# Multi-query attention on one core: TensorE's rounds of scores and value products follow the five-step period of the vector steps

## The chip, the cores and the metric

The kernel runs on one core of a Trainium2 chip. The metric is the device time in microseconds of one execution. Engine names in the profile: PE is TensorE (PEld its weight loads), ACT is ScalarE, DVE is VectorE, POOL is GpSimd, SP is SyncE.

## The reference

Attention with 16 query heads and one shared key and value head, for 8 batches of 1,024 tokens with head size 64:

```python
q = q.transpose(0, 2, 1, 3)                       # 8 x 16 x 1024 x 64
scores = np.matmul(q, k.transpose(0, 1, 3, 2)) / np.sqrt(head_dim)
weights = np.exp(scores - np.max(scores, axis=-1, keepdims=True))
weights = weights / np.sum(weights, axis=-1, keepdims=True)
attn_out = np.matmul(weights, v)                  # back to 8 x 1024 x 16 x 64
```

## The kernel before

The work is cut into 1,024 **steps** (`STEPS`). A step is one pair of heads, one chunk of 512 queries and one tile of 128 keys. Eight steps over the eight key tiles make a **chunk**; two chunks make a pair of heads, eight pairs a batch.

In a step, `scores` (L241) runs two matmuls on TensorE (L247), one for each head, which use the two halves of the array's rows side by side. They fill a PSUM tile `sc` of 128 keys by 1,024. The pool `scp` has three such tiles, so the scores of step u wait until the exponentials of step u-3 have been read out of theirs. No maximum is subtracted: a check at the end of each batch tests that the row sums stay in bounds.

The exponentials of a step are made by one of two units. In most steps ScalarE makes them in one instruction (L260). Every fifth step (`VE_EVERY = 5`, steps 10, 15, 20 and so on to 1005) is a **vector step**: VectorE makes them in five instructions (`vector_exp`, L206). The first (L211) reads the scores; the others (L217, L227, L235, L237) follow from the list `pend`, from which each step takes up to two entries. The fifth (L237) is put off until the next vector step. A vector step leaves its weights as three terms, each with its own scaled copy of the values.

The **value products** (`values`, L307, matmul L318) then multiply the weights, as the stationary operand, with the values (65 columns; the last one sums the weights). One **group** is one head's block of 128 queries; a chunk has eight groups. A group's sum runs over the eight key tiles, one product for a step by ScalarE and three for a vector step. A chunk with one vector step has 10 products a group, with two it has 12; three chunks in five have two. Seven groups share a PSUM bank (`ot`), of which there are two. When a bank is full, `late` notes it; VectorE then inverts the sums (`inverse`, L263) and scales the outputs (`finish`, L272), and SyncE's queue stores them. Some of the finishes end a batch and run the check too (L360, L366, L370).

The order on each engine is the order in which the program is written (`tc.manual_schedule`). The main loop (L448) goes by rounds of two steps: two steps' scores on TensorE, then two groups of value products, `LAG` = 18 steps behind. So a vector step is now the first, now the second step of a round, with a pattern that repeats every ten steps. From step 1012 (`HURRY`) on a round takes up to four groups. At the head of a round's value part, banks noted in the round before are put into `pend`. The last eight groups are done key tile by key tile at the end (`last_values`, L331, matmul L344), in two banks from the same pool. `after` (L392) issues the next batch's loads and transposes on POOL's and SP's queues.

Of the kernel before, what the change touches and what calls it, by code (L numbers as in the profile page):

```python
# [21 lines left out]
C0 = 0.9833984375  # L22
C3 = 0.163818359375
CS = 2.1471603163479376
VE_EVERY = 5


@with_exitstack
def attention_main(ctx, tc, q, k, v, out, flag):
# [14 lines left out]
    NKT = S // P  # L44
    QCH = 512
    NCH = S // QCH
    HP = H // 2
    NP = B * HP
    NQB = QCH // P
    GRP = 2 * NQB  # L50
    NG = NP * NCH * GRP
    GB = 7
# [25 lines left out]
    kv = {}  # L78
    q16 = {}
    qt = {}  # L80
    wt = {}
    osb = {}
    ot = {}
    pend = []
    product = []
    late = []
# [48 lines left out]
    def bank(name):  # L135
        return op.tile([P, 512], FP32, tag="ot", name=name)
# [32 lines left out]
    def first_q(ps, p, cs):  # L169
        for c in cs:  # L170
            nc.tensor.matmul(  # L171
                ps[:, c * P : (c + 1) * P],
                q16[("first", p)][:, c, :],
                ident16,
                is_transpose=True,
                start=True,
                stop=True,
            )
# [62 lines left out]
    def scores(p, c, j, by_vector):  # L241
# [17 lines left out]
        wt[(p, c, j)] = [(w, 0)]  # L259
        nc.scalar.activation(out=w, in_=sc, func=EXP, scale=escale, bias=math.log(CS))  # L260

    def inverse(o, g0, n):
        nc.vector.reciprocal(out=rec_all[:, g0 : g0 + n], in_=o[:, 0:n, D])  # L263

    def finish(o, g0, n):

        rec = rec_all[:, g0 : g0 + n]
        i0 = g0 % (OCH * GRP)
        if i0 == 0:
            osb[0] = osbp.tile([P, OCH * GRP, D], FP32, tag="osb", name=f"osb{g0}")  # L270
        ob = osb[0]
        nc.vector.tensor_tensor(  # L272
            out=ob[:, i0 : i0 + n, :],
            in0=o[:, 0:n, 0:D],
            in1=rec.unsqueeze(2).broadcast_to([P, n, D]),
            op=ALU.mult,
        )
        while stored[0] < g0 + n:
            e = stored[0]
            e += GRP // 2 if e >= NG - GRP else GRP  # L280
            if e > g0 + n:
                break
            store(ob, stored[0], e)
            stored[0] = e
        per = HP * NCH * GRP
        if g0 + n == NG:
            check(g0 - GRP // 2, NG, ok_all[:, B:])
        elif checked[0] < B and g0 + n >= min((checked[0] + 1) * per, NG - GRP):
            e = min((checked[0] + 1) * per, NG - GRP)
            b = checked[0]  # L290
            check(b * per, e, None, ok_all[:, b : b + 1])
            checked[0] += 1

    def store(ob, g0, g1):
        p, c = divmod(g0 // GRP, NCH)
        b, hp = divmod(p, HP)
        q0 = c * QCH + g0 % GRP // 2 * P
        j0 = g0 % (OCH * GRP)
        n = g1 - g0
        nc.sync.dma_start(  # L300
            out=out[b, q0 : q0 + n // 2 * P, 2 * hp : 2 * hp + 2, :].rearrange(
                "(qb p) h d -> p qb (h d)", p=P
            ),
            in_=ob[:, j0 : j0 + n, :].rearrange("p (qb h) d -> p qb (h d)", h=2),
        )

    def values(p, c, g):  # L307

        b = p // HP
        qb, hh = divmod(g, 2)  # L310
        gg = (p * NCH + c) * GRP + g
        if gg % GB == 0:
            ot[0] = bank(f"ot{gg}")[:, 0 : GB * 72].rearrange("p (g f) -> p g f", f=72)
        o = ot[0]
        vp = kv[b]["vp"]
        terms = [(j, w, i) for j in range(NKT) for w, i in wt[(p, c, j)]]
        for n, (j, w, i) in enumerate(terms):
            nc.tensor.matmul(  # L318
                o[:, gg % GB, 0 : D + 1],
                w[:, hh, qb * P : (qb + 1) * P],  # L320
                vp[:, i, j, 0 : D + 1],
                start=(n == 0),
                stop=(n == len(terms) - 1),
            )
        if gg % GB == GB - 1 or gg == NG - GRP - 1:
            late.append((o, gg - gg % GB, gg % GB + 1))
        if g == GRP - 1:
            for j in range(NKT):
                del wt[(p, c, j)]

    def last_values():  # L331

# [39 lines left out]
    LAG = 2 * NKT + 2  # L372
    STEPS = NP * NCH * NKT
    PSTEPS = NCH * NKT
    BATCH = 2
    LAST_VE = (STEPS - 2 * NKT) // VE_EVERY * VE_EVERY
    HURRY = STEPS - NKT - 4

    def to_vector(u):
        return u % VE_EVERY == 0 and NKT <= u <= LAST_VE  # L380

    def step(u):
        p, r = divmod(u, PSTEPS)
        c, j = divmod(r, NKT)
        scores(p, c, j, to_vector(u))
        for _ in range(2):
            if pend:
                pend.pop(0)()
        if product and u >= LAST_VE + 2 and not pend:
            product.pop()()  # L390

    def after(u):  # L392
        p, r = divmod(u, PSTEPS)
        b, hp = divmod(p, HP)
        if u == 1:
            first_q(turned[0], 0, range(NKT // 2, NKT))
            first_q_out(turned[0], 0, range(NKT // 2, NKT), nc.vector.tensor_copy)
        if r == 7 and p + 1 < NFIRST:
            turned[p + 1] = bank(f"qps{p + 1}").bitcast(FP16)
            first_q(turned[p + 1], p + 1, range(NKT))  # L400
            first_q_out(turned[p + 1], p + 1, range(NKT), nc.vector.tensor_copy)
        if b + 1 < B:
            at = hp * PSTEPS + r - 3 * PSTEPS
            if at == 0:
                load_kv(b + 1)
                load_v(b + 1)
            if 0 <= at < 2 * NKT and at % 2 == 0:
                load_q(b + 1, at // 2)
            at -= PSTEPS
            if 0 <= at < 2 * NKT and at % 2 == 0:  # L410
                turn_q(b + 1, at // 2)
            at -= PSTEPS
            if at == 4:
                prep_k(b + 1)
            if at == 8:
                prep_v(b + 1)

    with tc.manual_schedule():
        load_kv(0)
        load_q_first(0)  # L420
        make_identity(nc, ident)
        for p in range(1, NFIRST):
            load_q_first(p)
        load_v(0)
        for c in range(NKT):
            load_q(0, c)
        for t in vps:
            for i, ci in enumerate((1.0, C0, C3)):
                nc.gpsimd.memset(t[:, i, :, D : D + 1], ci)
        nc.vector.tensor_copy(out=ident16, in_=ident)  # L430
        nc.vector.memset(ones, 1.0)
        kps = bank("kps0").bitcast(FP16)
        turned[0] = bank("qps0").bitcast(FP16)
        lo, hi = range(NKT // 2), range(NKT // 2, NKT)
        q0 = q16[("first", 0)]
        nc.scalar.copy(out=q0[:, 0 : NKT // 2, :], in_=qf[:, 0 : NKT // 2, :])  # L436
        first_k(kps, 0)
        first_q(turned[0], 0, lo)
        first_q_out(turned[0], 0, lo, nc.scalar.copy)
        first_k_out(kps, 0)  # L440
        first_k(kps, 1)
        first_k_out(kps, 1)
        nc.vector.tensor_copy(out=q0[:, NKT // 2 :, :], in_=qf[:, NKT // 2 :, :])
        prep_v(0)
        for c in range(NKT):
            turn_q(0, c)
        nxt = 0
        for u0 in range(0, STEPS, BATCH):  # L448
            us = range(u0, u0 + BATCH)
            for u in us:  # L450
                step(u)
            for f in late:
                pend.insert(0, lambda f=f: inverse(*f))
                pend.insert(min(2, len(pend)), lambda f=f: finish(*f))
            del late[:]
            for _ in range(2 * BATCH):
                if u0 < HURRY:
                    ready = nxt < u0 + BATCH - LAG
                else:
                    ready = nxt < STEPS - GRP and nxt // GRP * NKT + NKT + 4 <= u0  # L460
                if ready:
                    pa, ra = divmod(nxt, PSTEPS)
                    values(pa, *divmod(ra, NKT))
                    nxt += 1
            for u in us:
                after(u)
        assert nxt == STEPS - GRP
        assert not product
        for f in pend:
            f()  # L470
        for f in late:
            inverse(*f)
            finish(*f)
        last_values()
        okm = chkp.tile([P, 1], FP32, tag="okm", name="okm")
        nc.vector.tensor_reduce(out=okm, in_=ok_all, axis=AX.X, op=ALU.min)
        cnt = bank("cnt")[0:1, 0:1]
        nc.tensor.matmul(cnt, okm, ones, start=True, stop=True)
        nc.vector.tensor_scalar(
            out=flag, in0=cnt, scalar1=P - 0.5, scalar2=None, op0=ALU.is_lt  # L480
        )
# [120 lines left out]
```

## Time and profile before

| | |
|---|---|
| Median of 3 runs | 782.43 us (781.96 to 783.74) |
| The profiled execution's own time | 783.46 us |
| Its span, first to last instruction | 781.5 us |
| ScalarE (ACT) busy | 762.5 us, 98% |
| VectorE (DVE) busy | 728.9 us, 93% |
| TensorE (PE) busy | 728.7 us, 93% |
| Granted TensorE clock, mean | 0.990 |
| Exponentials on ScalarE | 824, mean 1,062 ns |
| Vector steps | 200 |

The page is of one profiled execution. A row of a group of instructions gives its line, engine and operation, output and input, then the count, and behind the bar the busy time in us, the mean time of one in ns, and the idle time of the engine just before such instructions with what ended most of it. Exponentials follow each other so closely that one starts before the profile's end of the one before, so busy time over count is less than the mean. A timeline row gives start and length in us and merges instructions of a kind that follow without a gap.

### The profile page before, as it was taken

To read this page: it belongs to the slowest core of one execution; us is meant where nothing else is said; L and a number is where in the kernel's file an instruction comes from. 1 tells how busy PE (TensorE), PEld (TensorE's weight loads), DVE (VectorE), ACT (ScalarE), POOL (GpSimd) and SP (SyncE) were. 2 spreads that over 40 slices of the span, in tenths; PEclk is the share of its full clock that TensorE was granted. 3 is DMA by queue.
4 is the path that set the end of the run, shared out by engine and by line. 5 is a ranking of instruction groups with operands and counts; after the bars stand their busy time and mean duration, and the time that the engine had idled before them with its cause. 6 is when DMAs were issued, how large, how long until landed. Compare 5 with 4: busy or idle time off the path is not lost.

```text
span 781.5 us, 30669 instructions
## 1 busy us (share of the span) xinstructions
PE 728.7 (93%) x13474; PEld 474.1 (61%) x13474; DVE 728.9 (93%) x1349; ACT 762.5 (98%) x827; POOL 65.9 (8%) x99
## 2 busy tenths in 40 slices
PE   5999999999999999999999999999999999999996
PEld 2566666656666666666656666666666666666665
DVE  3899999999999999999999999999999999999992
ACT  7999999999999999999999999999999999999996
POOL 4210002100011002010020100201002100000000
PEclk8899999999999999999999999999999999999999
DMA  9949118582193813756155552556417373111113
GB/s 169 146 93 164 55 44 157 97 136 57 29 170 76 154 33 76 150 103 115 45 91 123 124 95 56 90 128 115 101 42 125 89 149 71 51 35 55 43 43 84
DMA packets 168633, 73.84 MB, mean 94 GB/s; under 512 B 93744, under 2 KB 161328, under 8 KB 168496
## 3 DMA queue, kind: packets, MB, share of 16 engines
q1 hardware_dynamic: 148864, 53.76, 32.5%
q0 software_dynamic: 18576, 17.57, 14.8%
q8 instruction: 106, 1.74, 1.0%
q10 hardware_dynamic: 1056, 0.52, 0.3%
q14 instruction: 31, 0.25, 0.1%
HBM read 37.75 MB, written 33.55 MB: 91 GB/s over the span
## 4 chain that ended last, share of the span: by engine, by line
ACT 38%; DVE 21%; PE 21%; issue 19%; DMA 1%; DVEq 0%; ACTq 0%
ACT wt L260 38%; PE ot L318 11%; PE sc L247 9%; DVE we L211 8%; DVE osb L272 3%; DVE we L237 3%; DVE mm L235 3%; DVE m L217 2%; DVE we L227 2%; DVE rec_all L263 1%; DMA qf<-in_q_dram 1%; PE otl L344 0%; DVE both L366 0%; DVE ok_all L370 0%; DVE ge L360 0%
## 5 line engine op out<-in xcount | busy, mean ns | idle before, releaser
L260 ACT ACTIVATE wt<-sc 128x1024 f16<-128x1024 f32 x824 | 760.0, 1062 | 7.4 <-PE sc L247 6.1
L318 PE MATMUL ot<-vp,wt 128*128 128x65 f16 x6528 | 418.4, 194 | 0.6 <-issue 0.6
L318 PEld LDWEIGHTS <-wt 128*128 128x128 f16 x6528 | 325.8, 98 | 114.8 <-issue 114.8
L247 PE MATMUL sc<-qt,k2t 64*128 64x512 f16 x2048 | 352.8, 386 | 41.2 <-ACT wt L260 29.1
L318 PE MATMUL ot<-vp,we 128*128 128x65 f16 x4800 | 352.2, 193 | 0.0
L318 PEld LDWEIGHTS <-we 128*128 128x128 f16 x4800 | 250.0, 97 | 30.6 <-issue 30.6
L211 DVE TENSOR_SCALAR we<-sc 128x1024 int16<-128x1024 f32 x200 | 243.6, 1218 | 23.2 <-PE sc L247 22.1
L247 PEld LDWEIGHTS <-k2t 64*128 64x128 f16 x2048 | 93.2, 94 | 149.0 <-issue 111.0
L237 DVE TENSOR_TENSOR we<-we,mm 128x1024 f16<-128x1024 f16 x200 | 136.9, 685 | 0.0
L235 DVE TENSOR_TENSOR mm<-m 128x1024 f16<-128x1024 f16 x200 | 136.5, 683 | 0.0
L272 DVE TENSOR_TENSOR osb<-ot,rec_all 128x448 f32<-128x448 f32 x146 | 90.5, 620 | 4.2 <-DVE rec_all L263 0.2
L217 DVE TENSOR_SCALAR m<-we 128x1024 int16<-128x1024 int16 x200 | 85.8, 429 | 0.0
L227 DVE TENSOR_SCALAR we<-we 128x1024 int16<-128x1024 int16 x200 | 83.5, 418 | 0.0
L104 POOL DMA_DIRECT2D vp<-in_v_dram x8 | 7.5, 936 | 388.5 <-PE ot L318 388.4
L121 POOL DMA_DIRECT2D q<-in_q_dram x64 | 35.0, 571 | 26.7 <-DMA qt<-q 22.9
L263 DVE RECIPROCAL rec_all<-ot 128x7 f32<-128x7 f32 x146 | 28.6, 196 | 8.7 <-PE ot L318 8.6
L190 POOL TENSOR_SCALAR k16d<-knat 128x512 f16<-128x512 f32 x14 | 21.4, 1537 | 134.7 <-DMA knat<-in_k_dram 134.7
L202 DVE TENSOR_SCALAR vp<-vp 128x512 f16<-128x512 f16 x16 | 3.9, 286 | 2.0 <-DMA vp<-in_v_dram 2.0
L155 PE MATMUL kps<-ident,k 128*64 128x128 f16 x16 | 1.3, 314 | 4.5 <-DVE k L146 4.5
L184 DVE COPY qt<-qps 128x512 f16<-128x512 f16 (+1 forms) x2 | 1.1, 554 | 3.3 <-PE qps L171 3.3
L155 PEld LDWEIGHTS <-k 128*64 128x64 f16 x16 | 0.8, 159 | 4.7 <-DVE k L146 4.7
L436 ACT ACT_TABLE_LOAD x1 | 1.3, 1283 | 1.9 <-issue 1.9
(29 smaller groups left out, 22.2 us busy)
## 6 DMA issues: line engine op xcount, KB each, us to landing
out_dram<-osb SPq DMA_DIRECT2D x127, 256.0 KB, 2.4
q<-in_q_dram POOLq DMA_DIRECT2D x56, 256.0 KB, 8.8
knat<-in_k_dram SPq DMA_DIRECT2D x7, 256.0 KB, 4.1
q<-in_q_dram POOLq DMA_DIRECT2D x8, 192.0 KB, 8.0
vp<-in_v_dram POOLq DMA_DIRECT2D x8, 128.0 KB, 4.4
qt<-q SPq DMA_TRANSPOSE x64, 3.9
qf<-in_q_dram ACTq DMA_DIRECT2D x2, 256.0 KB, 4.4
knat<-in_k_dram SPq DMA_DIRECT2D x2, 128.0 KB, 3.8
```

Of the source, the lines that this page charges most:

```text
L121: nc.gpsimd.dma_start(out=q16[(b, c)], in_=q[b, c * P : (c + 1) * P, h0:, :].rearrange("p h d -> p (h d)"),)
L190: nc.gpsimd.tensor_scalar(out=k16d[:, :, i, :], in0=st["knat"], scalar1=kscale, scalar2=None, op0=ALU.mult)
L211: nc.vector.tensor_scalar(out=t, in0=sc, scalar1=15.0 * 1024, scalar2=0.0, op0=ALU.add, op1=ALU.max)
L217: lambda: nc.vector.tensor_scalar(out=m.bitcast(I16), in0=t, scalar1=0x3FF, scalar2=0x3C00, op0=ALU.bitwise_and, op1=ALU.bitwise_or,)
L227: lambda: nc.vector.tensor_scalar(out=w3[:, 0].bitcast(I16), in0=t, scalar1=0x7C00, scalar2=None, op0=ALU.bitwise_and,)
L235: pend.append(lambda: nc.vector.tensor_tensor(out=m2, in0=m, in1=m, op=ALU.mult))
L237: lambda: nc.vector.tensor_tensor(out=w3[:, 2], in0=w3[:, 1], in1=m2, op=ALU.mult)
L247: nc.tensor.matmul(sc[:, hh, :], k2t[r : r + 64, j * P : (j + 1) * P], qt[b][r : r + 64, p % HP, c * QCH : (c + 1) * QCH], start=True, sto ...
L260: nc.scalar.activation(out=w, in_=sc, func=EXP, scale=escale, bias=math.log(CS))
L263: nc.vector.reciprocal(out=rec_all[:, g0 : g0 + n], in_=o[:, 0:n, D])
L272: nc.vector.tensor_tensor(out=ob[:, i0 : i0 + n, :], in0=o[:, 0:n, 0:D], in1=rec.unsqueeze(2).broadcast_to([P, n, D]), op=ALU.mult,)
L318: nc.tensor.matmul(o[:, gg % GB, 0 : D + 1], w[:, hh, qb * P : (qb + 1) * P], vp[:, i, j, 0 : D + 1], start=(n == 0), stop=(n == len(terms ...
```

## The change

Three things change. First, the rounds no longer have two steps each. `DEAL` and `DEAL_AT` place the end of a round behind steps 1, 2 and 4 of each five, counted from a vector step: the vector step and the next one make a round, one step alone the second, the last two the third. Second, the rounds' value work is no longer counted in groups. `values` returns a list of single products, and `plan` works out how many products shall have been made by each round's end, so that the three rounds of a period have the same share of five groups; a group can be cut by the next round's scores. At the end of a period one group more is made than before at the same step. Third, `HURRY` is 1010 instead of 1012, and from there on rounds of two steps with up to four whole groups take a chunk's groups up two steps earlier than before.

```diff
+DEAL = (1, 1, 0, 1, 0)
+DEAL_AT = 1
 VE_EVERY = 5
...
-    def values(p, c, g):
+    def values(gg):
...
-        for n, (j, w, i) in enumerate(terms):
+        def one(n, j, w, i):
+            last = n == len(terms) - 1
             nc.tensor.matmul(
...
+        return [lambda n=n, t=t: one(n, *t) for n, t in enumerate(terms)]
...
-    BATCH = 2
-    HURRY = STEPS - NKT - 4
+    HURRY = STEPS - NKT - 6
...
+    def plan():
+        upto = [0]
+        for g in range(STEPS):
+            many = sum(to_vector(g // GRP * NKT + j) for j in range(NKT))
+            upto.append(upto[-1] + NKT + 2 * many)
+        due = {}
+        for u in range(STEPS):
+            if u >= HURRY:
+                if u % 2:
+                    due[u] = None
+                continue
+            n, i = divmod(u - DEAL_AT, len(DEAL))
+            if DEAL[i]:
+                at = DEAL_AT + len(DEAL) * (n + sum(DEAL[: i + 1]) / sum(DEAL)) - LAG
+                at = max(at, 0.0)
+                g = int(at)
+                due[u] = round(upto[g] + (at - g) * (upto[g + 1] - upto[g]))
+        return due
...
-        for u0 in range(0, STEPS, BATCH):
-            us = range(u0, u0 + BATCH)
-            for u in us:
-                step(u)
+        for u in range(STEPS):
+            step(u)
+            us.append(u)
+            if u not in due:
+                continue
+            new = []
             for f in late:
-                pend.insert(0, lambda f=f: inverse(*f))
-                pend.insert(min(2, len(pend)), lambda f=f: finish(*f))
+                new += [lambda f=f: inverse(*f), lambda f=f: finish(*f)]
+            if len(new) == 2:
+                new[1:1] = pend[:1]
+                del pend[:1]
+            pend[:0] = new
             del late[:]
-            for _ in range(2 * BATCH):
-                if u0 < HURRY:
-                    ready = nxt < u0 + BATCH - LAG
-                else:
-                    ready = nxt < STEPS - GRP and nxt // GRP * NKT + NKT + 4 <= u0
-                if ready:
-                    pa, ra = divmod(nxt, PSTEPS)
-                    values(pa, *divmod(ra, NKT))
-                    nxt += 1
+            if due[u] is not None:
+                while made < due[u]:
+                    if not todo:
+                        todo = values(nxt)
+                        nxt += 1
+                    todo.pop(0)()
+                    made += 1
+            else:
+                for _ in range(4):
+                    if not todo and nxt < STEPS - GRP and nxt // GRP * NKT + NKT + 3 <= u:
+                        todo = values(nxt)
+                        nxt += 1
...
```

More of the change, by code (lines that the diff above doesn't have):

```diff
@@ L305, in store @@
         )
-    def values(p, c, g):
-        b = p // HP
+    def values(gg):
+        p, c = divmod(gg // GRP, NCH)
+        g = gg % GRP
         qb, hh = divmod(g, 2)
-        gg = (p * NCH + c) * GRP + g
         if gg % GB == 0:
@@ L314, in values @@
         o = ot[0]
-        vp = kv[b]["vp"]
+        vp = kv[p // HP]["vp"]
         terms = [(j, w, i) for j in range(NKT) for w, i in wt[(p, c, j)]]
-        for n, (j, w, i) in enumerate(terms):
+        def one(n, j, w, i):
+            last = n == len(terms) - 1
             nc.tensor.matmul(
@@ L322, in values @@
                 start=(n == 0),
-                stop=(n == len(terms) - 1),
+                stop=last,
             )
[L325 to L329, printed above, removed]
+            if not last:
+                return
+            if gg % GB == GB - 1 or gg == NG - GRP - 1:
+                late.append((o, gg - gg % GB, gg % GB + 1))
+            if g == GRP - 1:
+                for x in range(NKT):
+                    del wt[(p, c, x)]
+        return [lambda n=n, t=t: one(n, *t) for n, t in enumerate(terms)]
     def last_values():
@@ L446, in attention_main @@
             turn_q(0, c)
-        nxt = 0
-        for u0 in range(0, STEPS, BATCH):
-            us = range(u0, u0 + BATCH)
-            for u in us:
-                step(u)
-            for f in late:
-                pend.insert(0, lambda f=f: inverse(*f))
-                pend.insert(min(2, len(pend)), lambda f=f: finish(*f))
-            del late[:]
-            for _ in range(2 * BATCH):
-                if u0 < HURRY:
-                    ready = nxt < u0 + BATCH - LAG
-                else:
-                    ready = nxt < STEPS - GRP and nxt // GRP * NKT + NKT + 4 <= u0
-                if ready:
-                    pa, ra = divmod(nxt, PSTEPS)
-                    values(pa, *divmod(ra, NKT))
-                    nxt += 1
-            for u in us:
-                after(u)
+        nxt = made = 0
+        todo = []
+        due = plan()
+        us = []
+        for u in range(STEPS):
[4 more added lines that the diff above has]
+            new = []
+            for f in late:
+                new += [lambda f=f: inverse(*f), lambda f=f: finish(*f)]
[3 more added lines that the diff above has]
+            pend[:0] = new
+            del late[:]
+            if due[u] is not None:
[10 more added lines that the diff above has]
+                        nxt += 1
+                    for f in todo:
+                        f()
+                    todo = []
+            for x in us:
+                after(x)
+            us = []
         assert nxt == STEPS - GRP
```

## The prediction

> **What bounds the kernel now.** I read the page first, for the shares of the engines and the costliest groups.
>
> ```profile
> PE 728.7 (93%) x13474; PEld 474.1 (61%) x13474; DVE 728.9 (93%) x1349; ACT 762.5 (98%) x827; POOL 65.9 (8%) x99
> ...
> L260 ACT ACTIVATE wt<-sc 128x1024 f16<-128x1024 f32 x824 | 760.0, 1062 | 7.4 <-PE sc L247 6.1
> ...
> L247 PE MATMUL sc<-qt,k2t 64*128 64x512 f16 x2048 | 352.8, 386 | 41.2 <-ACT wt L260 29.1
> ```
>
> Three engines look full, ScalarE most. Its exponentials overlap (mean 1.06 us, but 760.0/824 = 0.92 each), so the question is how close it runs to its own floor. The timeline of ScalarE merges exponentials without a gap into one row; columns are start, length, and in brackets the idle time before.
>
> ```profile
> 7.35 17.55 ACT L260 ACTIVATE wt<-sc 128x1024 f16<-128x1024 f32 x19 [0.70 <-PE sc L247]
> ...
> 230.09 182.66 ACT L260 ACTIVATE wt<-sc 128x1024 f16<-128x1024 f32 x198 [0.24 <-PE sc L247]
> ...
> 728.03 45.97 ACT L260 ACTIVATE wt<-sc 128x1024 f16<-128x1024 f32 x50 [0.21 <-PE sc L247]
> ```
>
> The last row gives the floor: (45.97 - 1.07) / 49 = 0.9163; end to end in the trace nearly all lie at 0.914 to 0.918, so I use 0.9165. From 7.35 to the end of the last at 774.00 is 766.65 us; 823 x 0.9165 + 1.02 = 755.3. So **11.3 us** is all that smoother feeding can return. Adding up in the trace what each exponential's end lies over 0.9165 behind the one before: about 1.5 falls before step 43 (0.75 at steps 21 and 22, still at the slower clock (the first slices of the page's PEclk row read 8), 0.8 at step 42 behind a pause in the value products that nothing releases); about 4.1 in clusters some 128 steps apart, where VectorE runs a batch's check and comes late; 5.7 is the rest, nearly all at steps 6 mod 10: a vector step is the second of a round there, so ScalarE gets one step from that round and starves through the next values.
>
> **The pieces of a period.** VectorE and TensorE rows, start and length (matmul ends are modelled, so I use starts):
>
> ```profile
> 302.40 0.20 DVE L263 RECIPROCAL rec_all<-ot 128x7 f32<-128x7 f32 x1
> ...
> 303.18 1.21 DVE L211 TENSOR_SCALAR we<-sc 128x1024 int16<-128x1024 f32 x1
> ...
> 306.18 0.20 DVE L263 RECIPROCAL rec_all<-ot 128x7 f32<-128x7 f32 x1
> ```
>
> ```profile
> 233.00 0.39 PE L247 MATMUL sc<-qt,k2t 64*128 64x512 f16 x2 [0.17 <-ACT wt L260]
> 233.32 0.27 PE L318 MATMUL ot<-vp,we 128*128 128x65 f16 x3
> ...
> 234.16 0.61 PE L247 MATMUL sc<-qt,k2t 64*128 64x512 f16 x4
> 234.70 0.27 PE L318 MATMUL ot<-vp,we 128*128 128x65 f16 x3
> ...
> 235.55 0.60 PE L247 MATMUL sc<-qt,k2t 64*128 64x512 f16 x4
> ```
>
> A finish (inverse and scaling) costs VectorE 0.78, a vector step's five operations 3.00. On TensorE a waited step's scores stand 0.32 before the first value product; two steps' scores 0.54, of which 0.22 lies between the two, so 0.31 follows the second. 24 products and the change back to scores take 0.85: 0.031 a product, 0.13 from the last product to the scores. In the trace a step's scores start 0.05 after the end of the exponential that frees their buffer, an idle ScalarE starts 0.49 after the scores (VectorE 0.43), and its exponential then takes 1.02.
>
> **Part 1: rounds of two, one, two with equal shares.** Nothing is added or removed: 2,048 score matmuls, 11,328 + 64 value products, the same vector work. The built order shows the split as meant: the vector step opens a two-step round, a lone step follows, then two, with 16 to 20 products behind each.
>
> *TensorE.* Three rounds a period for two and a half. In chunks with two vector steps (12 products a group, three chunks in five) a period holds 60 products: before 60 x 0.031 + 2.5 x (0.22 + 0.31 + 0.10) = 3.44 us, after 1.86 + 2 x 0.22 + 3 x 0.41 = 3.53 (0.10 is the change back less a product's own 0.03; 0.41 is 0.31 + 0.10). The floor is 4 x 0.9165 = 3.67, which hides the added 0.09 (18 us over 203 periods if that cover were gone).
>
> *The tightest loop.* Call the steps of a period 0 (the vector step) to 4. There are three score buffers, so step 1's scores wait for the exponential of step 3 of the period before. Set step 1's scores at 0. Values from 0.32, 20 products 0.59, change 0.13: the lone step 2 at 1.04. Values from 1.35, again 0.59 and 0.13: step 3's scores at 2.07. Its exponential starts at 2.56, ends at 3.58, frees the buffer at 3.63. That is under 3.67 by 0.03, so ScalarE sets the period even here; with 10 products a group (16 to 17 a round) 0.2 more is free. The trace has no lone step that did not wait. Its change to values lies between 0.31 (second of two) and 0.32 (waited); the far row is 0.54 at the slower clock (scores 21.25, values 21.80). I take 0.31, the nearest; anything lower gains nothing, since the loop is under the floor already. The far row would add 0.23: 0.20 over the floor in 122 of 203 periods, 24 us.
>
> *VectorE.* Five finishes in seven periods: 3.00 + 0.78 x 5/7 = 3.56 against 3.67. Now that vector steps are evenly spaced, its lateness grows by 0.11 in each of at most three finish periods in a row, then falls by 0.67: at most 0.33. The scores of step 3 wait for the vector step's first operation (1.22): scores of the vector step at -0.34, start 0.09, free at 1.36 plus the lateness, against 2.07. Cover 0.71, enough. A check adds 0.77 (0.24 + 0.33 + 0.20 in the trace): lateness up to 1.1, some 0.4 over the cover; seven checks at 0.43 make 3.0, for 4.1 now. Scaled values of a batch add 0.4, just covered. The output banks: a finish stands behind the vector step's fourth operation or behind the first; the tightest of the five phases ends 0.39 less the lateness before TensorE needs the bank, and that phase's lateness is 0.11. If that cover went, every 0.1 beyond would cost 29 x 0.1 us.
>
> *Start.* Values begin at step 17 instead of 19, while TensorE is still at the slower clock (products 0.054, change 0.54): about 0.8 more waiting, 2.3 in all with the pause of 0.8 kept.
>
> Sum: 2.3 + 3.0 + 1.0 (scaled values, neighbours, what I missed) = 6.3 for 11.3: **-5.0 us**, between +0.8 (only the start changes) and -9.8.
>
> **Part 2: the end.** The chain of waits shows what follows the last exponential:
>
> ```profile
> 772.96 0.64 DVE osb L272
> ...
> 773.98 1.89 PE otl L344 x56
> ...
> 775.89 0.19 DVE rec_all L263
> ```
>
> The last loop products ran behind the last scores, to 772.6; their finish held the banks until 773.6, and 60 of the 64 last products then ran, almost all after the last exponential (773.99). After the change groups 1012 to 1015 come before step 1022's scores, about 3 us before the last exponential ends; two finishes later (about 1.4) the banks are free, 52 or so products (1.6) fit in before that end, and only the last eight must follow (0.25 + 0.15). Inverse 0.4 after the last exponential, not 1.9: **-1.5 us**, from 0 (should the finishes come late) to -1.7. The fullest round (48 products, step 1015) brings step 1016's scores just in time, so the exponentials keep their pace. POOL's and SP's issues move by a step at most and have no row on the chain here.
>
> **Sum.** Profiled execution 783.46 (span 781.5 and 1.96 around it): 783.46 - 5.0 - 1.5 = 777.0. The median of runs is 782.43, 1.03 below it: **775.9 us**.
>
> **Rivals.**
> *Only the end improves.* Gaps move to other steps, because VectorE's lateness makes them. For it: clusters with scores held by VectorE. Against it: 5.7 us stand at one phase of the rounds. Time 782.43 - 1.5 = 780.9. A rule of the Trainium skill leads there too: ScalarE: Activation LUTs, "What ACT_TABLE_LOAD costs", gives an ACTIVATE with immediates 186 ns + 0.833 ns per element and an overlap of 93 ns; an estimate from it is 0.946 each, 779.5 for 824, so no gap at all would be left to close. The trace disagrees: 0.916 over 50 in a row. Chance 0.11.
> *Slower: the lone step's round.* If the two changes around a lone step cost 0.10 more than I took, the tightest loop is 3.73, 0.07 over the floor in 122 of 203 periods: 8.5 us, and the shares behind leave no room to catch up. 775.9 + 8.5 = 784.4. From about 0.09 on the time passes the one before; the far row's 24 us would give 800. Against it: the waited step's 0.32, which has nothing else in flight. Chance 0.14.
> *All but the start goes.* If checks fit the cover too: 2.3 left, 782.43 - 9.0 - 1.5 = 771.9. Chance 0.13.
> That the rounds are not as described can be ruled out by the built order.
>
> **Numbers.** Forecast 0.62, the rest as above. A measurement can tell about 0.2% (1.6 us). Faster: 0.61 of the forecast, 0.13, and 0.02 of the first rival: 0.76; same 0.10; slower 0.14. Range 771.5 to 783.5: it leaves out most of the slower case and a little at the foot.
>
> **What would show it.** Right: ScalarE's merged runs get longer and its first start to last end falls from 766.7 to about 762 us; value rows in threes of 16 to 20 products; the inverse about 0.4 after the last exponential. Wrong: scores of step 3 late behind VectorE in many periods, a lone step whose values start over 0.4 behind it, values waiting for scaling (L272), or exponential gaps every five steps.

## The result and the profile after

The changed kernel takes 775.67 us (median of 6 runs, 773.22 to 778.12), against 782.89 us before on the same occasions (6 runs, 781.96 to 783.98). The ratio is 0.9902, with a 95% interval of 0.9884 to 0.992. The profiled execution took 773.22 us with a span of 771.4 us; it is the fastest of its six, so its trace shows the change at its best.

The page of the changed kernel, the rows that answer to those of before:

```profile
PE 744.1 (96%) x13474; PEld 471.9 (61%) x13474; DVE 730.3 (95%) x1349; ACT 759.3 (98%) x827; POOL 66.9 (9%) x99
...
L262 ACT ACTIVATE wt<-sc 128x1024 f16<-128x1024 f32 x824 | 756.8, 1085 | 2.0 <-PE sc L249 1.7
...
L249 PE MATMUL sc<-qt,k2t 64*128 64x512 f16 x2048 | 364.6, 388 | 16.2 <-ACT wt L262 12.1
```

ScalarE is idle for 2.0 us before its exponentials instead of 7.4. Its mean exponential reads longer, 1,085 for 1,062 ns, while the busy time falls: with fewer gaps more of each lies over its neighbour, so the mean says nothing here and the runs of the timeline do. TensorE's busy time is 15.4 us more, with the same 13,474 matmuls. That fits the added half change per period (18 us was estimated), and ScalarE's gaps show no cost of it.

The timeline of ScalarE after (start, length, idle before):

```profile
7.23 16.84 ACT L262 ACTIVATE wt<-sc 128x1024 f16<-128x1024 f32 x18 [0.70 <-PE sc L249]
24.30 475.77 ACT L262 ACTIVATE wt<-sc 128x1024 f16<-128x1024 f32 x518 [0.23 <-PE sc L249]
500.45 98.19 ACT L262 ACTIVATE wt<-sc 128x1024 f16<-128x1024 f32 x107 [0.38 <-PE sc L249]
599.00 166.36 ACT L262 ACTIVATE wt<-sc 128x1024 f16<-128x1024 f32 x181 [0.35 <-PE sc L249]
```

There were 19 such runs; there are 4. The second row is 518 exponentials at (475.77 - 1.07) / 517 = 0.918 us, almost the floor of 0.9165. From 7.23 to the end of the last exponential, 765.36, is 758.1 us, where 755.3 is the floor: 2.8 us lost instead of 11.3.

TensorE in a period of 12-product groups (start, length; the first row holds the vector step's scores and those of step 1):

```profile
232.56 0.71 PE L249 MATMUL sc<-qt,k2t 64*128 64x512 f16 x4
233.21 0.24 PE L323 MATMUL ot<-vp,wt 128*128 128x65 f16 x2
...
233.93 0.39 PE L249 MATMUL sc<-qt,k2t 64*128 64x512 f16 x2
234.25 0.20 PE L323 MATMUL ot<-vp,wt 128*128 128x65 f16 x1
...
234.97 0.61 PE L249 MATMUL sc<-qt,k2t 64*128 64x512 f16 x4
235.51 0.20 PE L323 MATMUL ot<-vp,we 128*128 128x65 f16 x1
```

This is the tightest loop of the prediction. Step 1's scores start at 232.89 in the trace, the lone step at 233.93 (1.04 later), step 3 at 234.97 (1.04). Its exponential starts at 235.46 and ends at 236.50, and the scores of the next period's step 1 start at 236.55. That is 3.67 for the loop.

The chain of waits at the end:

```profile
762.68 0.64 DVE osb L274
...
763.70 2.02 PE otl L353 x56
765.72 0.02 issue
765.74 0.19 DVE rec_all L265
```

The banks are free at 763.3 and the last exponential ends at 765.36, so all but eight of the last products run before it. The inverse follows 0.4 us behind it. Before, it was 1.9.

The two profiled executions differ by 10.2 us: 8.5 in the gaps between exponentials, 1.5 at the end, 0.1 ahead of the first exponential. Of the 8.5, 0.9 lies before step 45, and that much is not shown to be the change's: the profile before lost 1.5 there, but the two kernels below that keep the old rounds and change only the end lost 0.6 and 0.1. Behind step 45 the gaps fall from 9.9 to 2.2. The medians differ by 7.2.

### The profile page after: what moved, and what is told of

It reads as the page before. It is cut to its first block, busy times and chain, and to the rows that moved or that the text cites. A ratio compares the mean times of both kernels' runs of the same rounds, so it can differ in the third digit from the quotient of the medians.

```text
span 771.4 us, 30670 instructions
## 1 busy us (share of the span) xinstructions
PE 744.1 (96%) x13474; PEld 471.9 (61%) x13474; DVE 730.3 (95%) x1349; ACT 759.3 (98%) x827; POOL 66.9 (9%) x99
## 4 chain that ended last, share of the span: by engine, by line
PE 40%; ACT 35%; issue 12%; DVE 12%; DMA 1%; ACTq 0%; DVEq 0%
ACT wt L262 35%; PE ot L323 22%; PE sc L249 18%; DVE we L213 4%; DVE osb L274 2%; DVE we L239 2%; DVE mm L237 2%; DVE we L229 1%; DVE m L219 1%; DMA qf<-in_q_dram 1%; DVE rec_all L265 0%; PE otl L353 0%; DVE both L375 0%; DVE ok_all L379 0%; DVE ge L369 0%
## 5 line engine op out<-in xcount | busy, mean ns | idle before, releaser
L262 ACT ACTIVATE wt<-sc 128x1024 f16<-128x1024 f32 x824 | 756.8, 1085 | 2.0 <-PE sc L249 1.7
L323 PE MATMUL ot<-vp,wt 128*128 128x65 f16 x6528 | 430.1, 194 | 0.8 <-DVE osb L274 0.8
L249 PE MATMUL sc<-qt,k2t 64*128 64x512 f16 x2048 | 364.6, 388 | 16.2 <-ACT wt L262 12.1
L249 PEld LDWEIGHTS <-k2t 64*128 64x128 f16 x2048 | 86.3, 94 | 108.7 <-issue 75.7
L229 DVE TENSOR_SCALAR we<-we 128x1024 int16<-128x1024 int16 x200 | 85.3, 426 | 0.0
```

Source lines behind the costliest of these rows:

```text
L229: lambda: nc.vector.tensor_scalar(out=w3[:, 0].bitcast(I16), in0=t, scalar1=0x7C00, scalar2=None, op0=ALU.bitwise_and,)
L249: nc.tensor.matmul(sc[:, hh, :], k2t[r : r + 64, j * P : (j + 1) * P], qt[b][r : r + 64, p % HP, c * QCH : (c + 1) * QCH], start=True, sto ...
L323: nc.tensor.matmul(o[:, gg % GB, 0 : D + 1], w[:, hh, qb * P : (qb + 1) * P], vp[:, i, j, 0 : D + 1], start=(n == 0), stop=last,)
```

## The experiments

Theory A is the prediction's: ScalarE's floor of 3.67 us per period holds unless a chain through a score buffer, value work and an exponential (or VectorE's first operation) is longer. Theory B holds that small, even portions of value work between the scores help, wherever the lone step stands. Ratios are to the kernel before, run on the same chip.

### The two parts apart

**The rounds without the new end.** The edit to the changed kernel:

```diff
-    HURRY = STEPS - NKT - 6
+    HURRY = STEPS - NKT - 4
...
-                    if not todo and nxt < STEPS - GRP and nxt // GRP * NKT + NKT + 3 <= u:
+                    if not todo and nxt < STEPS - GRP and nxt // GRP * NKT + NKT + 4 <= u - 1:
```

> The changed rounds of two, one, two with equal shares, but the end of the kernel by the old rule (from step 1012, two steps later). Theory A (chains of waits: ScalarE's floor of 4 x 0.9165 = 3.67 us per period holds unless a chain through a score buffer, value work and an exponential is longer, and the place of the lone step decides that) takes the end as a separate 1.5 us: about 777.2, a ratio of 0.9927 to before, the last inversion about 1.9 us behind the last exponential. If the rounds alone do it all (the end hidden anyway): 775.7. If the end rule were needed for the rest too: over 779.

775.67 us, ratio 0.9909 (0.9893 to 0.9926). In time that is the second expectation, but the kernel before took 782.12 on this chip, 0.8 less than beside the change; by the ratio it lies between the first (0.9927) and the change (0.9902). The trace decides: the last exponential ends at 767.34 us and the inverse starts at 769.24, 1.9 behind it, so the end is not hidden. The gaps sum to 4.8 us, of which 2.3 stand before step 52 (0.6 up to step 23, 1.1 at steps 42 and 43, 0.6 at step 51).

**The end without the rounds, first try.** The edit to the kernel before:

```diff
-    HURRY = STEPS - NKT - 4
+    HURRY = STEPS - NKT - 6
...
-                    ready = nxt < STEPS - GRP and nxt // GRP * NKT + NKT + 4 <= u0
+                    ready = nxt < STEPS - GRP and nxt // GRP * NKT + NKT + 3 <= u0 + 1
```

> The rounds of two as before, with the new rule for the end alone (groups taken up from step 1010 and two steps earlier). Theory A: only the stretch behind the last exponential shrinks, by 1.5 us: 781.4, a ratio of 0.998; the last inversion 0.4 us behind the last exponential, the gaps before it unchanged at about 11 us. Rival: the end costs nothing in its place, 782.9.

781.67 us, ratio 0.9996 (0.9986 to 1.0006): no gain, but the end is not alone in this kernel. Two full banks now come due at once, and the old way of queueing puts the second one's finish first, so the last outputs are stored unscaled. The chain shows the check of a batch in front of the finish that frees the bank:

```profile
770.94 0.15 DVE osb L272
771.10 0.14 DVE ge L360
771.26 0.29 DVE both L366
...
771.88 0.63 DVE osb L272
...
772.56 1.87 PE otl L344 x56
```

**The end without the rounds, finishes in order.** As above, with the changed kernel's lines for `new`.

> The rounds of two as before, with the new rule for the end and with the change's way of queueing two finishes in their order (the kernel end_only queued the last two full banks' finishes in swapped order, so its last outputs are stored unscaled and the check ran between them). Theory A: the last inversion 0.4 us behind the last exponential instead of 1.9, all else as before: 0.998, 781.4 for 782.9. Rival: earlier groups in the last rounds make the exponentials wait (0.3 us at step 1018 in end_only) and the finishes still hold the banks: no gain, 782.9.

781.48 us for 782.46, ratio 0.9983 (0.9974 to 0.9992). The last exponential ends at 773.53; the chain goes on:

```profile
770.98 0.64 DVE osb L272
...
771.99 1.91 PE otl L344 x56
773.90 0.02 issue
773.92 0.19 DVE rec_all L263
```

The inverse follows 0.4 us behind. The end alone is worth 1.0 us in time, 1.5 in its stretch. Of the rest, 0.28 went back where the rival said: the last rounds of 48 products make the exponential of step 1018 wait that long here.

### Where the lone step stands

**The lone step last.**

```diff
-DEAL = (1, 1, 0, 1, 0)
+DEAL = (1, 0, 1, 1, 0)
```

> As the change, but the lone step is the period's last: rounds of the vector step and the next, then two, then one; shares still equal. Theory A: the third step after the vector step now waits for VectorE's first operation (0.43 + 1.22 + 0.05 = 1.70 after the vector step's scores), then two rounds' values lie before the next vector step (1.04 + 1.03): 3.77 per period with 12 products a group, and 3.72 with 10 once finishes push VectorE back. That is 0.10 x 122 + 0.06 x 81 = 17 us more than the change: about 793, slower than before. Theory B (even, smaller portions of value work between scores are what helps, wherever the lone step stands): 774 to 778.

799.40 us, ratio 1.0219 (1.02 to 1.0237). Theory B falls. Theory A has the sign and the place, but 6 us too little. The waits of this kernel (us in total, times, longest):

```profile
DVE we L213 <- PE sc L249: 34.9, 57, 1.8
PE sc L249 <- DVE we L213: 26.5, 79, 1.0
```

Scores waiting for VectorE's first operation were 7.6 us in 19 waits before. The chain of 3.77 was right for a period in which VectorE is on time. From step 1's scores to the next period's, 49 periods hold 60 products: the 14 with no finish between the vector step and the one before it took 3.79 to 3.80 each, the other 35 took 3.90 on average and up to 4.65. Here VectorE is itself in the chain, so a finish that makes it late costs time; my sum counted that only with 10 products a group. That VectorE is late there is in the rows; how the excess splits into finishes, checks and scalings is not shown.

**The vector step alone.** Edit: `DEAL_AT = 0` and `DEAL = (1, 0, 1, 0, 1)`.

> As the change, but the lone step is the vector step itself, then two rounds of two; shares equal. Theory A: a chain over two periods rules with 12 products a group: the fourth exponential frees the buffer for step 2 (0.05), values (1.04), the pair 3 and 4 (0.22), values (1.03), the vector step, values (1.03), step 1 and its exponential (1.51), three more exponentials (2.75): 7.64 for two periods, 3.82 each, 0.15 over the floor in 122 periods: 19 us more than the change, less the checks, which would then be covered (2): about 792. Theory B: 774 to 778.

793.40 us, ratio 1.0142 (1.0122 to 1.0162), against 792 expected. Scores of steps 1 and 2 on TensorE in three periods of this trace (each row merges the two steps):

```profile
236.01 0.84 PE L249 MATMUL sc<-qt,k2t 64*128 64x512 f16 x4
...
239.81 0.92 PE L249 MATMUL sc<-qt,k2t 64*128 64x512 f16 x4
...
243.66 0.85 PE L249 MATMUL sc<-qt,k2t 64*128 64x512 f16 x4
```

A period is 3.80, then 3.85: 7.65 for two, where the chain over two periods gave 7.64.

**The lone step behind the vector step.** Edit: `DEAL_AT = 0`, the rest as changed; values then follow steps 0, 1 and 3.

> As the change, but the lone step is the one behind the vector step, and the vector step closes a two-step round with the step before it: values behind steps 0, 1 and 3 of each period; equal shares. Theory A: no chain passes the floor here either, since the tightest one again holds two shares, two changes and one exponential (3.63 against 3.67): the same as the change within 1 us, 774 to 776. Rival C (what helps is that the vector step opens a round, so that ScalarE gets a step from every round; the two other places were slow for that reason): rounds that give ScalarE one step and then a vector step starve it as before the change, 782 or more.

773.80 us, ratio 0.9885 (0.9869 to 0.9901), the same as the change within the intervals. Rival C falls: the vector step closes a round here, as it did in half of the rounds before, and ScalarE does not starve. The prediction gave that place in the round as the cause of 5.7 us of gaps, so the place alone is not enough; what else it took is said under "Why the prediction was right".

### Whole groups, and their shares

Both kernels keep the changed rounds and deal whole groups: `DEAL = (2, 1, 0, 2, 0)` for two, one, two, and `(2, 2, 0, 1, 0)` for two, two, one.

> As the change, but the three rounds of a period deal whole groups, two, one, two, and no group is cut by scores. Theory A: the two rounds that lie in the tightest chain hold 36 products instead of 40, the third 24, no chain passes the floor: same as the change, within 1 us (775.7). Theory B (equal small portions, dealt singly, are what helps): up to 24 products stand between scores again, as before the change; half of the gain lost, about 779.

774.26 us, ratio 0.9898 (0.9883 to 0.9913), where the change itself, beside it, had 0.9893. Dealing products singly is worth nothing that can be measured.

> As the one before with the shares two, two, one: the two rounds of the tightest chain hold 48 products with 12 a group. Theory A: 0.05 + 0.32 + 23 x 0.031 + 0.13, then 0.31 + 23 x 0.031 + 0.13, then 0.49 + 1.02 is 3.88 per period, 0.22 over the floor in 122 periods: 26 us more than the change, about 801, slower than before by over 2%; the 81 other periods at the floor. Theory B: the same as the shares two, one, two.

800.73 us, ratio 1.0235 (1.0219 to 1.025), against 801 expected. The rows of one loop:

```profile
237.46 0.39 PE L249 MATMUL sc<-qt,k2t 64*128 64x512 f16 x2 [0.16 <-ACT wt L262]
...
238.62 0.39 PE L249 MATMUL sc<-qt,k2t 64*128 64x512 f16 x2
...
239.79 0.61 PE L249 MATMUL sc<-qt,k2t 64*128 64x512 f16 x4
...
241.35 0.39 PE L249 MATMUL sc<-qt,k2t 64*128 64x512 f16 x2 [0.17 <-ACT wt L262]
```

From step 1's scores to the next period's it is 3.89 us, in two rounds of 24 products (1.16 and 1.17) and one exponential; 3.88 was worked out. The wait in the brackets is ScalarE's: TensorE waits for the very exponential that it made late. The two kernels have the same rounds and the same work, and differ by 26.5 us through 12 products that stand in another round.

### The change again, and VectorE's checks

> The changed kernel itself, for a second profile and beside the variants on the same chip. 775.7 (773 to 778). If the scatter between its executions comes from how early TensorE's clock is granted in the first 25 us, an execution over 775.5 shows a lower clock in the first two stretches of 20 us and more waiting before step 45, with the middle unchanged; if it comes from VectorE's checks and neighbours, the start is alike and the clusters differ.

774.32 us, ratio 0.9893 (0.9878 to 0.9908). The profiled execution took 774.07, and its gaps sum to 3.65 us: 1.3 before step 45 and 2.4 behind, where the first profile had 0.6 and 2.2. TensorE between 22 and 26 us, in the first profile and then in this one (x13 and x14 are value products):

```profile
22.44 0.90 PE L323 MATMUL ot<-vp,wt 128*128 128x65 f16 x13
...
24.19 0.59 PE L323 MATMUL ot<-vp,wt 128*128 128x65 f16 x13
```

```profile
22.37 0.90 PE L323 MATMUL ot<-vp,wt 128*128 128x65 f16 x13
...
24.17 0.89 PE L323 MATMUL ot<-vp,wt 128*128 128x65 f16 x13
24.99 0.61 PE L249 MATMUL sc<-qt,k2t 64*128 64x512 f16 x2
25.53 0.83 PE L323 MATMUL ot<-vp,wt 128*128 128x65 f16 x14
```

The products start 0.054 us apart at first and 0.03 later; the second pace has begun by 24.2 us in the first profile and by 26.1 in this one. Of the 0.85 us between the two executions 0.7 lies at the start, 0.6 of it at steps 22 and 23, just where TensorE is still at the first pace in one and not in the other. The old rounds show the same at step 22: 0.04, 0.56 and 0.62 us lost where the second pace has begun by 24.0 (the end alone, in order), 25.4 (its first try) and 26.0 (the kernel before). The granted clock of the page is no help here: for the first profile it reads 1.00 from the start (0.81 and 0.85 in the first two stretches of 20 us here), but that trace has no record of the clock before 24.1 us, and its products are just as slow up to 23.0.

That is not all: the kernel with the rounds alone reached the second pace by 24.3 us too and still lost 1.6 at steps 42, 43 and 51. No execution of the change over 775.5 us was profiled, so the scatter of 5 us between its runs stays open.

**The checks put off.** `finish` puts a batch's check into a list `spare`, and a step takes it from there:

```diff
+        if spare and u % VE_EVERY == VE_EVERY - 1 and finished[1] < u - VE_EVERY + 1 and not pend:
+            spare.pop(0)()
```

where `finished[1]` is the step of the last finish.

> As the change, but a batch's check (0.77 us of VectorE) is put off to the end of the next period without a finish, in which VectorE has 0.66 us to spare. Theory A: VectorE's lateness stays under the cover of 0.71, the clusters at the checks go (1.5 to 2 us in the profile of the change): 773.9. If those clusters come from something else at the batch's border (neighbouring loads, scaled values), no change: 775.7.

773.09 us, ratio 0.988 (0.9863 to 0.9897). Against 774.32 for the change on the same chip that is 1.2 us less, but the intervals overlap, so the time alone does not show it. The timeline of ScalarE does:

```profile
25.79 739.41 ACT L264 ACTIVATE wt<-sc 128x1024 f16<-128x1024 f32 x805 [0.18 <-PE sc L251]
```

From 25.79 us on it has no idle time; what is lost behind step 45 falls from 2.4 to about 1.2 us. In this profile and the change's second one 0.8 of that is a small excess spread over all exponentials; the clusters fall from 1.6 to 0.4, and those that remain are at steps 818 and 823. The checks in their old place were the cause of the other clusters. By its median this is the fastest kernel of the study, though its interval overlaps those of the change and of two variants.

## Why the prediction was right

**The floor.** 11.3 us at most to return, from exponentials 0.9165 apart: right. The change's trace comes within 2.8 of it, and no kernel went below. The rival with the rule of the Trainium skill (ScalarE: Activation LUTs, "What ACT_TABLE_LOAD costs"; estimate 0.946 per exponential) falls: 518 in a row took 0.918 each, and the whole span from the first to the last, 758.1, is less than the 779.5 that the rule asks for.

**What starved ScalarE before.** The prediction put 5.7 us on a place in the round: a vector step that closes a round leaves ScalarE one step. The profile before shows that this needed VectorE to be late as well:

```profile
173.60 1.22 DVE L211 TENSOR_SCALAR we<-sc 128x1024 int16<-128x1024 f32 x1
...
174.87 0.39 PE L247 MATMUL sc<-qt,k2t 64*128 64x512 f16 x2 [0.40 <-DVE we L211]
...
177.91 1.02 ACT L260 ACTIVATE wt<-sc 128x1024 f16<-128x1024 f32 x1 [0.36 <-PE sc L247]
```

VectorE starts vector step 220 0.6 us later than the 0.43 behind its scores that an idle VectorE takes; step 223's scores wait for it, and the exponential of step 226 is late. Of the 94 steps 6 mod 10 from 56 to 986, 26 lose more than 0.1 us (6.8 together, some of it in what the prediction counted as clusters), and in all 26 VectorE had started the vector step six steps earlier at least 0.11 late, with step 3's scores 0.05 behind the end of its first operation. Where it was less than 0.1 late (64 times) none lost more than 0.06; the other four were late and lost nothing. So the first rival was right that VectorE's lateness makes the gaps, and wrong that they only move. What the new rounds gave is the cover: in the periods that start at a multiple of ten, step 3's scores start 0.05 us behind the end of VectorE's first operation before (median) and 0.60 after, and TensorE's waits for that operation fall from 7.6 us to 1.0. The variant with the lone step last has 0.05 again.

**The loops.** TensorE's added half change per period stays hidden: 15.4 us more busy time, none in the span. The tightest loop was worked out at 3.63 and measures at most 3.67 (it then waits for ScalarE). Its lone step's change to values, the unknown between 0.31 and 0.54, is 0.32. The two kernels made to break a loop of ScalarE came out within 2 us (792 and 801 expected, 793.40 and 800.73 measured), and the kernel with two, one and two whole groups, whose portions are uneven, is as fast as the change; so the loop, not the portion, is the mechanism. The third, which put VectorE into the loop, was 6 us off, as said.

**VectorE.** Here the sizes were off. Lateness at most 0.33 without checks: in the trace a quarter of the vector steps are over 0.42 late, and one behind a check, step 280, starts 1.6 late:

```profile
213.69 0.39 PE L249 MATMUL sc<-qt,k2t 64*128 64x512 f16 x2
...
214.95 0.22 DVE L369 TENSOR_SCALAR ge<-rec_all 128x128 f32<-128x128 f32 x1
...
215.53 0.28 DVE L379 TENSOR_REDUCE ok_all<-both 128x1 f32<-128x128 f32 x1
215.73 1.22 DVE L213 TENSOR_SCALAR we<-sc 128x1024 int16<-128x1024 f32 x1
```

My 0.71 for the cover was also too low just there. By the semaphores in the trace the scores that wait for VectorE's first operation are step 3's after 195 of the 200 vector steps, but step 4's after five of the seven checks (steps 159, 284, 544, 799 and 924). Step 4's exponential comes one exponential, 0.92 us, after step 3's, so there is more room. The clusters behind the checks cost about 1.9 us instead of 3.0.

**The start.** 2.3 us was the most wrong term: 0.6 and 1.3 in the two profiles of the change. The pause of 0.8 that I kept from before did not occur in them, though it did, with 0.9 at step 42, in the kernel with the rounds alone. The added waiting was forecast at 0.8: in the second profile of the change, where the first pace lasts as long as before, it is 0.6 (1.3 in all, where the profile before has 0.65 without its pause). **The remainder** of 1.0 was about 0.4.

**The end.** -1.5 us was exact in the trace (1.9 to 0.4 behind the last exponential). The slow rounds of 48 products that I said would come just in time cost nothing in the change (no step from 1006 on loses 0.01 us), but 0.28 where the old rounds run before them and 0.20 with the lone step behind the vector step.

**The sum.** On the profiled execution's scale I had 777.0 and it was 773.22; on the median's scale 775.9, and it was 775.67. The second agreement is in part luck. The terms for start, checks and remainder were together 3.5 too large for the fastest execution, and the median lies 2.45 above that one, while before it lay 1.0 below its profiled one. Which execution each profile happened to show shifted my sum by as much as its errors.

## What to carry to other kernels

When several engines look full, find the floor of the one that is bound (end to end in its longest gapless run) and what it loses above it; then write down the chains that go through each buffer and back, period by period, and over two periods where one does not close. How much work stands between two waits matters only in the chain that is longest: the same rounds with 12 products moved cost 26 us. Work that comes seldom, such as a check, belongs in the period in which its engine has time to spare.

## What the runs showed that I had not expected

The rows of ScalarE start 0.903 us apart inside a run but end 0.9165 apart, and the lengths grow from 1.02 to 1.16 until the start gap gives in; the starts alone would have given a floor 11 us too low over the kernel. And a pool of three score buffers does not always hand them out in turn: after five checks of the changed kernel, and of the one with the lone step last, the scores that wait for VectorE are those of step 4 and not of step 3. In the kernel before, and with the checks put off, they are step 3's after all 200 vector steps.
